# The second gate's modulation, computed in 64 small pieces on VectorE: each piece tied to its chunk's last low part, with four buffers and loads three chunks ahead

## The chip, the cores and the metric

The kernel runs on one core of one Trainium2 chip. The metric is the device time of one execution, in microseconds, so lower is better. The engines are called PE (TensorE's matrix products), PEld (its weight loads), DVE (VectorE), ACT (ScalarE), POOL (GpSimd) and SP (SyncE, which only issues transfers here). Each engine works through its own instructions in a fixed order.

## What is computed

One layer of a transformer-like block on x of shape 512 x 2048, with a feed-forward width of 5632, all in float32. The part that matters here is the modulation `mod`, a product of one vector with a 2048 x 12288 matrix that yields six vectors of 2048, and the end of the layer, where the sixth of them, gt2, multiplies the result of the feed-forward part.

```
c_act = jax.nn.silu(c)
...
mod = c_act @ w_ada[l] + b_ada[l]
sh1, sc1, gt1, sh2, sc2, gt2 = jnp.split(mod, 6, axis=-1)
h = modulate(rms_norm(x, g_mix[l]), sh1, sc1)
...                    # input projection, two head groups, output projection
x = x + gt1 * ...
h = modulate(rms_norm(x, g_ffn[l]), sh2, sc2)
...                    # up projection of width 2 x 5632, SiLU gate, down projection
x = x + gt2 * ...
```

## The kernel before, in words

The kernel goes through its stages one behind the other: the mixing part (until 742 us), two ordinary up units and 40 fast up units (742 to 1668 us), and the down projection (1668 to 2099 us). A product in float32 is made of three: every operand is split into a high part (made on ACT) and a low part (the rest, made on DVE), and PE computes high by high, high by low and low by high.

**Fast up units.** A unit uf{f}, f = 4 to 43, makes one 128-wide slice of the gate and of the up projection by a scheme of the Strassen kind with seven products where there would be eight. It consists of two chunks (c = 0, 1) with 84 matmuls each. `fast_chunk` prepares the weights of a chunk, uq{f}_{c}: SP loads them raw (L1037, `r`), ACT makes the high parts and DVE the low parts of four groups, named `a`, `c`, `s` and `t` in the order in which PE uses them (`ah`/`al` and so on; L229 and L230 in `wsplit`, L1043 and L1044 for `c`), and DVE makes the sums between them (L1046, L1047, L1050). The last low part of a chunk is `tl`. High and low parts of the groups a, s and t have three buffers each, so the weights are made about a chunk ahead of PE. At the end of a unit ACT copies one product from PSUM (L1083, uw), DVE combines the seven (L1084 to L1088), ACT applies SiLU (L1089), DVE multiplies gate and up (L1090, ug), and `keep_act` makes the combinations that the down projection needs (L961 to L964) and SP writes them to DRAM as td (L965 to L969). POOL meanwhile adds weight blocks of the down projection in DRAM (L977).

**The pieces of gt2.** The sixth modulation vector is spread over the fast up units from unit 12 on, one piece per chunk, 64 pieces in all (`gt2_piece`, called behind a chunk's matmuls are written). A piece is a load of 256 KB of the matrix (L173, on ACT's queue, so that it stands in line with ACT's high parts) and one operation on DVE that multiplies it by the vector c and adds up along each row (L182). The tiles have two buffers, and the load of piece n + 2 is written behind the operation of piece n. Behind the last piece, four small sums on DVE (L188, L190) put the four quarters together with the bias into `mod`. At the start of the down projection, `gt2_spread` turns the vector round: SP scatters it to DRAM as gt2d (L1152, 8 KB in elements of 4 bytes), and four broadcast loads bring it back as gt2b (L1156), which is first used near the end.

**Down projection.** Each chunk of a phase loads a block of weights (L1100, `dq…r`) and activations from td (L1115, `dq…tl`); ACT makes the high part of the activations (L1116, `th`) and of the weights (L229, `w0h`, `w1h`), and DVE the low parts (L1117, L230) and a sum of two weight blocks (L1122). In the first phase products 4 and 5 alternate, so two chunks share every name, such as dq_0tl: the first is product 4's and the second product 5's. PE's groups are called dn4, dn5 and so on.

**What sets the order.** A scheduler orders each engine's instructions by priority and dependencies. `tc.high_priority(offset=AHEAD)` raises the priority of what is written in it; weights of chunks ahead are written in it. `tc.issue_after(i)` makes an instruction stand behind instruction i. `tail_hi` and `tail_lo` are lists of ACT's high parts and DVE's low parts, to which `wsplit` appends; `tail_lo[-1]` is the last low part written so far, which at a piece is its chunk's `tl`.

Of the kernel before, what the change touches and what calls it, by code (L numbers as in the profile page):

```python
# [8 lines left out]
F32 = mybir.dt.float32  # L9
F32R = mybir.dt.float32r  # L10
AF = mybir.ActivationFunctionType
ALU = mybir.AluOpType
AX = mybir.AxisListType

P = 128
D = 2048
S = 512
KT = D // P
# [18 lines left out]
AHEAD = 2000  # L37
# [27 lines left out]
def block_kernel(ctx, tc, xT, crow, adaT, vecs, bfr, w1, wyr, wqkv0, wqkv, wgate, wout, wup0, wups, wdn, outT):  # L65
    nc = tc.nc
    PSUM = bass.MemoryType.PSUM
    cp = ctx.enter_context(tc.tile_pool(name="cp", bufs=1))
# [13 lines left out]
    def page(name, tag, shape=None):  # L82
        return pgp.tile(shape or [P, S], F32, tag=tag, name=name, bufs=TAGS[tag])
# [13 lines left out]
    c_b = cp.tile([P, D], F32, name="c_b")  # L97
# [69 lines left out]
    gt2_acc = cp.tile([P, 4, KT], F32, name="gt2_acc")  # L167
    gt2_src = {}

    def gt2_load(n):  # L170
        t = cp.tile([P, S], F32, name=f"gt2_{n}", tag="ssq", bufs=2)
        with tc.issue_after(tail_hi[-1]):
            nc.scalar.dma_start(out=t, in_=adaT[GT2 * KT + n // 4, :, (n % 4) * S:(n % 4 + 1) * S])  # L173
        gt2_src[n] = t

    def gt2_piece(n):
        if n == 0:
            gt2_load(0)
            gt2_load(1)
        t = gt2_src.pop(n)  # L180
        r = n % 4
        nc.vector.scalar_tensor_tensor(out=t, in0=t, scalar=1.0, in1=c_b[:, r * S:(r + 1) * S], op0=ALU.mult, op1=ALU.mult,  # L182
                                       accum_out=gt2_acc[:, r, n // 4:n // 4 + 1])
        if n < 4 * KT - 2:
            gt2_load(n + 2)
        if n == 4 * KT - 1:
            m = mods[GT2]
            nc.vector.tensor_add(m, gt2_acc[:, 0, :], vec[:, V_BADA + GT2 * KT:V_BADA + (GT2 + 1) * KT])  # L188
            for r in range(1, 4):
                nc.vector.tensor_add(m, m, gt2_acc[:, r, :])  # L190
# [7 lines left out]
    tail_lo, tail_hi = [], []  # L198
# [167 lines left out]
    for kt in range(KT):  # L366
# [3 lines left out]
        else:  # L370
# [3 lines left out]
                                       in1=bg[:, kt:kt + 1], op0=ALU.add, op1=ALU.add)  # L374
# [19 lines left out]
    for f in (4, 5, 6, 7, 0, 1, 2, 3):  # L394
        t = page(f"xr{f}", "c")
# [35 lines left out]
    for f in range(4):  # L431
        t = page(f"yr{f}", "c")
# [437 lines left out]
    for g in range(4):  # L870
# [12 lines left out]
        for f in range(4):  # L883
            kt = g * 4 + f
            t = page(f"x1_{kt}", "c")
# [173 lines left out]
    for f in range(2 * STD, FT):  # L1059
        ps = [bank(f + 1, b, f"uf{f}p{b}") for b in range(4)]  # L1060
        m = {p: ps[b][:, h * HS:(h + 1) * HS] for p, (b, h) in where.items()}
        for c in range(2):
            for p, hi, lo in fast_chunk(f, c):
                for k in range(4):
                    th, tl = T[p][c * 4 + k]
                    ks = slice(k * P, (k + 1) * P)
                    for n, (w, x) in enumerate(((hi, th), (hi, tl), (lo, th))):
                        first, last = c + k + n == 0, c == 1 and k == 3 and n == 2
                        nc.tensor.matmul(m[p], lhsT=R(w[:, ks]), rhs=R(x), start=first and p in opens, stop=last,  # L1069
                                         skip_group_check=True)  # L1070
            if f == 2 * STD and c == 0:
                up_last()
            n = 2 * (f - 2 * STD) + c
            if 0 <= n - GT2_AT < 4 * KT:
                gt2_piece(n - GT2_AT)
            if 0 <= n - SUMS_AT < 6 * NQ and (n - SUMS_AT) % 6 < 4:
                sums24((n - SUMS_AT) // 6, (n - SUMS_AT) % 6)
# [28 lines left out]
    def dn_chunk(ph, q, hold=False):  # L1106
        prods = PHASES[ph]
        out = {p: [] for p, _, _ in prods}
        with tc.high_priority(offset=AHEAD):
            raws, ts = [], []  # L1110
            for n, (p, blk, ix) in enumerate(prods):
                nm = f"dq{p}_{q}"
                raws.append(dn_load("raw2" if n or (len(prods) == 1 and q % 2) else "raw", blk, q, nm + "r"))
                tl, th = page(nm + "tl", "h"), page(nm + "th", "h")
                nc.sync.dma_start(out=tl, in_=td[ph][q][:, ix])  # L1115
                nc.scalar.activation(R(th), tl, AF.Copy)  # L1116
                nc.vector.tensor_sub(R(tl), tl, th)  # L1117
                ts.append((th, tl))
            for n, (p, blk, ix) in enumerate(prods):
                nm, raw = f"dq{p}_{q}", raws[n]  # L1120
                if n and blk >= 0:
                    nc.vector.tensor_add(raw, raw, raws[0])  # L1122
                for k in range(2):
                    if hold and n == 0:
                        w = []
                        for i in range(2):
                            src = raw[:, (2 * k + i) * S:(2 * k + i + 1) * S]
                            hi, lo = page(f"{nm}h{k}{i}", "h"), page(f"{nm}l{k}{i}", "h")
                            nc.scalar.activation(R(hi), src, AF.Copy)
                            nc.vector.tensor_sub(R(lo), src, hi)  # L1130
                            w.append((hi, lo))
                    else:
                        hi, lo = wsplit(raw[:, k * 1024:(k + 1) * 1024], 1024, f"{nm}w{k}")
                        w = [(hi[:, i * S:(i + 1) * S], lo[:, i * S:(i + 1) * S]) for i in range(2)]
                    ks = slice(k * HS, (k + 1) * HS)
                    out[p].append((w, ts[n][0][:, ks], ts[n][1][:, ks]))
        return out
# [45 lines left out]
    for ph, prods in enumerate(PHASES):  # L1183
# [4 lines left out]
        for q in range(NQ):  # L1188
            hold = ph == 3 and q >= NQ - 2
            out = dn_chunk(ph, q, hold)  # L1190
# [101 lines left out]
```

## Time and profile before

| | us |
|---|---|
| median of 3 runs | 2101.8 (2100.73 to 2103.46) |
| profiled execution | 2100.19 |
| its span, first to last instruction | 2098.5 |
| PE busy in the span | 2047.3 (98%) |
| DVE busy | 1709.0 (81%) |
| ACT busy | 939.6 (45%) |
| the 64 pieces on DVE (L182), busy | 43.9 |
| from the first unit with pieces (uf12) to the last (uf43) | 1004.77 to 1643.66 |

Times inside the profile count from the start of its span. A group's row reads: line, engine, operation, output <- input, shape, count, then busy us and mean ns of one, then idle time of the engine just ahead of these and what ended it. A row of the chain of waits reads: start, length, what. A row of the waits reads: who waited <- for whom: us in all, times, longest.

### The profile page before, as it was taken

Reading aid. Unit: us, or ns where it says so; the run is one execution under the profiler, and the core shown is the slowest. Engines: PE = TensorE matmul, PEld = TensorE weight load, DVE = VectorE, ACT = ScalarE, POOL = GpSimd, SP = SyncE. Lnnn points to the kernel's source line nnn. Section 1 sums busy time; section 2 is a strip of 40 time slices with the busy share of each in tenths; the row PEclk is TensorE's granted clock in tenths of the full one; section 3 lists DMA queues with packets and bytes.
Section 4 is the critical chain, followed back from the end, with each engine's and each line's share of the span. In section 5 each row is a group of like instructions: output and inputs, shape, how many; then the busy total and the mean of one; then the engine's idle time right before and its main releaser. Section 6 shows DMA issues by size and latency. Waiting matters only on the chain.

```text
span 2098.5 us, 32298 instructions
## 1 busy us (share of the span) xinstructions
PE 2047.3 (98%) x12529; PEld 1856.8 (88%) x12529; DVE 1709.0 (81%) x2547; ACT 939.6 (45%) x1331; POOL 92.6 (4%) x111
## 2 busy tenths in 40 slices
PE   8999999999999999999999999999999999999999
PEld 6889898888788887999999999999999888888877
DVE  8999768987776569988798897889898877777785
ACT  4433447765433355444343333343343445545443
POOL 0000000000100000000000000000000000000000
PEclk9999999999999999999999999999999999999999
DMA  9989766667667532448878788987878587677884
GB/s 339 354 290 317 247 204 209 232 212 255 229 229 265 201 131 78 141 134 221 243 226 236 233 233 222 251 245 220 246 230 228 164 280 249 233 244 249 275 303 151
DMA packets 174044, 485.21 MB, mean 231 GB/s; under 512 B 20385, under 2 KB 45377, under 8 KB 169794
## 3 DMA queue, kind: packets, MB, share of 16 engines
q1 hardware_dynamic: 154530, 429.66, 60.6%
q0 software_dynamic: 10144, 36.70, 9.4%
q10 hardware_dynamic: 9216, 16.78, 2.4%
q8 instruction: 98, 1.61, 0.3%
q14 instruction: 56, 0.46, 0.1%
HBM read 447.40 MB, written 93.35 MB: 258 GB/s over the span
## 4 chain that ended last, share of the span: by engine, by line
PE 73%; DVE 13%; DMA 9%; issue 2%; ACT 2%; POOL 1%; SPq 0%; ACTq 0%; DVEq 0%
PE w1p L234 4%; DMA gt<-in_adaT 3%; PE dn6p L234 3%; PE dn7p L234 3%; PE dn1p L234 3%; PE yr1p L234 2%; PE up0p L234 2%; PE wo2p L234 2%; PE wo1p L234 2%; PE wo3p L234 2%; PE dn3p L234 2%; PE dn5p L234 2%; PE wo0p L234 2%; PE dn2p L234 2%; PE yr0p L234 2%
## 5 line engine op out<-in xcount | busy, mean ns | idle before, releaser
L229 ACT ACTIVATE uq_0sh<-uq_0r 128x1024 fp32r<-128x1024 f32 x40 | 42.4, 1060 | 221.6 <-DVE uq_0r L1047 221.6
L154 DVE SCALAR_TENSOR_TENSOR ada<-ada,c_b 128x1024 f32<-128x1024 f32 x96 | 115.9, 1219 | 26.3 <-DMA ada<-in_adaT 26.1
L182 DVE SCALAR_TENSOR_TENSOR gt<-gt,c_b 128x512 f32<-128x512 f32 x64 | 43.9, 685 | 61.3 <-DMA gt<-in_adaT 61.3
L229 ACT ACTIVATE uq_1sh<-uq_1r 128x1024 fp32r<-128x1024 f32 x40 | 42.5, 1062 | 106.4 <-DVE uq_1r L1047 95.5
L977 POOL DMA_DIRECT2D s2d<-in_wdn x44 | 36.4, 827 | 692.0 <-DMA s2d<-in_wdn 674.7
L230 DVE TENSOR_TENSOR uq_0sl<-uq_0r,uq_0sh 128x1024 fp32r<-128x1024 f32 x40 | 49.0, 1225 | 17.3 <-ACT uq_0sh L229 15.9
L229 ACT ACTIVATE uq_0ah<-uq_0r 128x1024 fp32r<-128x1024 f32 x40 | 42.2, 1056 | 34.4 <-PE uf8p L1069 1.8
L230 DVE TENSOR_TENSOR uq_0al<-uq_0r,uq_0ah 128x1024 fp32r<-128x1024 f32 x40 | 48.8, 1220 | 7.5 <-ACT uq_0ah L229 7.3
L230 DVE TENSOR_TENSOR uq_0tl<-uq_0r,uq_0th 128x1024 fp32r<-128x1024 f32 x40 | 48.8, 1219 | 7.6 <-ACT uq_0th L229 7.6
L1089 ACT ACTIVATE ug<-ug 128x512 f32<-128x512 f32 x40 | 25.3, 632 | 62.8 <-DVE ug L1086 62.8
L234 PE MATMUL w1p<-hph,w1h 128*128 128x512 f32 x128 | 46.9, 395 | 5.9 <-ACT hph L378 5.9
L229 ACT ACTIVATE uq_1ah<-uq_1r 128x1024 fp32r<-128x1024 f32 x40 | 42.2, 1055 | 20.1 <-issue 15.5
L230 DVE TENSOR_TENSOR uq_1tl<-uq_1r,uq_1th 128x1024 fp32r<-128x1024 f32 x40 | 48.8, 1219 | 2.5 <-ACT uq_1th L229 2.5
L234 PE MATMUL w1p<-hpl,w1h 128*128 128x512 f32 x128 | 50.6, 395 | 0.0
L234 PE MATMUL w1p<-hph,w1l 128*128 128x512 f32 x128 | 50.3, 393 | 0.0
L230 DVE TENSOR_TENSOR uq_1sl<-uq_1r,uq_1sh 128x1024 fp32r<-128x1024 f32 x40 | 48.8, 1220 | 0.0
L1046 DVE TENSOR_TENSOR uq_0r<-uq_0r 128x1024 f32<-128x1024 f32 x40 | 48.7, 1217 | 0.0
L230 DVE TENSOR_TENSOR uq_1al<-uq_1r,uq_1ah 128x1024 fp32r<-128x1024 f32 x40 | 48.6, 1214 | 0.0
L1046 DVE TENSOR_TENSOR uq_1r<-uq_1r 128x1024 f32<-128x1024 f32 x40 | 48.5, 1213 | 0.0
L229 ACT ACTIVATE uq_0th<-uq_0r 128x1024 fp32r<-128x1024 f32 x40 | 41.9, 1048 | 12.9 <-DVE uq_0r L1050 3.0
L229 ACT ACTIVATE uq_1th<-uq_1r 128x1024 fp32r<-128x1024 f32 x40 | 42.0, 1051 | 9.7 <-PE uf10p L1069 1.0
L164 DVE SCALAR_TENSOR_TENSOR ada<-ada,c_b 128x1024 f32<-128x1024 f32 x32 | 38.9, 1216 | 2.0 <-DMA ada<-in_adaT 2.0
(12770 smaller groups left out, 8149.7 us busy)
## 6 DMA issues: line engine op xcount, KB each, us to landing
ada<-in_adaT SPq DMA_DIRECT2D x128, 512.0 KB, 5.0
uq_1r<-in_wups SPq DMA_DIRECT2D x80, 512.0 KB, 8.3
uq_0r<-in_wups SPq DMA_DIRECT2D x80, 512.0 KB, 4.9
s2d<-in_wdn POOLq DMA_DIRECT2D x44, 512.0 KB, 9.4
adf<-in_adaT SPq DMA_DIRECT2D x32, 512.0 KB, 5.9
gt<-in_adaT ACTq DMA_DIRECT2D x64, 256.0 KB, 4.6
s2d<-in_wdn SPq DMA_DIRECT2D x22, 512.0 KB, 8.4
s4d<-in_wdn SPq DMA_DIRECT2D x22, 512.0 KB, 8.5
```

The costliest lines, as they stand in the source:

```text
L154: nc.vector.scalar_tensor_tensor(out=t, in0=t, scalar=1.0, in1=cs, op0=ALU.mult, op1=ALU.mult, accum_out=ac)
L164: nc.vector.scalar_tensor_tensor(out=t, in0=t, scalar=1.0, in1=c_b[:, cs], op0=ALU.mult, op1=ALU.mult, accum_out=ada_acc[j][:, hf, i:i + 1])
L182: nc.vector.scalar_tensor_tensor(out=t, in0=t, scalar=1.0, in1=c_b[:, r * S:(r + 1) * S], op0=ALU.mult, op1=ALU.mult, accum_out=gt2_acc[:, ...
L229: tail_hi.append(nc.scalar.activation(R(hi[:, :n]), raw_ap, AF.Copy).ins)
L230: tail_lo.append(nc.vector.tensor_sub(R(lo[:, :n]), raw_ap, hi[:, :n]).ins)
L234: nc.tensor.matmul(ps, lhsT=R(l), rhs=R(r), start=start, stop=stop)
L977: nc.gpsimd.dma_start(out=out[:, cs], in_=src[:, cs], accum_op=ALU.add)
L1046: nc.vector.tensor_add(blocks[:, 0:3:2], blocks[:, 0:2], blocks[:, 2:3].broadcast_to([P, 2, 512]))
L1089: nc.scalar.activation(g, g, AF.Silu)
```

## The change

The tiles of the pieces take two tags by turns, with two buffers each, so there are four. Three loads are issued at the first piece, and the load of piece n + 3 is written ahead of the operation of piece n. The operation itself is written with high priority and is tied to stand behind the last low part that was written. Nothing else is edited.

```
     def gt2_load(n):
-        t = cp.tile([P, S], F32, name=f"gt2_{n}", tag="ssq", bufs=2)
+        t = cp.tile([P, S], F32, name=f"gt2_{n}", tag=("ssq", "rstd_b")[n % 2], bufs=2)
...
     def gt2_piece(n):
-        if n == 0:
-            gt2_load(0)
-            gt2_load(1)
+        for k in range(3 if n == 0 else 0):
+            gt2_load(k)
+        if n < 4 * KT - 3:
+            gt2_load(n + 3)
         t = gt2_src.pop(n)
         r = n % 4
-        nc.vector.scalar_tensor_tensor(out=t, in0=t, scalar=1.0, in1=c_b[:, r * S:(r + 1) * S], op0=ALU.mult, op1=ALU.mult,
-                                       accum_out=gt2_acc[:, r, n // 4:n // 4 + 1])
-        if n < 4 * KT - 2:
-            gt2_load(n + 2)
+        with tc.issue_after(tail_lo[-1]), tc.high_priority(offset=AHEAD):
+            nc.vector.scalar_tensor_tensor(out=t, in0=t, scalar=1.0, in1=c_b[:, r * S:(r + 1) * S], op0=ALU.mult,
+                                           op1=ALU.mult, accum_out=gt2_acc[:, r, n // 4:n // 4 + 1])
```

How this moves instructions is shown at two places. The first is DVE's order around the end of unit 15 (uq15_1 is its second chunk; sl and tl are the last two low parts of a chunk, al the first). Before:

```order
L230 TENSOR_TENSOR uq15_1sl_10350<-uq15_1r_10336,uq15_1sh_10349 128x1024
L182 SCALAR_TENSOR_TENSOR gt2_8_10332,gt2_acc_128<-gt2_8_10332,c_b_81 128x512
L230 TENSOR_TENSOR uq15_1tl_10355<-uq15_1r_10336,uq15_1th_10354 128x1024
L182 SCALAR_TENSOR_TENSOR gt2_9_10443,gt2_acc_128<-gt2_9_10443,c_b_81 128x512
L230 TENSOR_TENSOR uq16_0al_10478<-uq16_0r_10474,uq16_0ah_10477 128x1024
```

And now:

```order
L230 TENSOR_TENSOR uq15_1sl_10352<-uq15_1r_10338,uq15_1sh_10351 128x1024
L1090 TENSOR_TENSOR ug14_10211<-ug14_10211,uu14_10212 128x512
L230 TENSOR_TENSOR uq15_1tl_10357<-uq15_1r_10338,uq15_1th_10356 128x1024
L184 SCALAR_TENSOR_TENSOR gt2_7_10093,gt2_acc_128<-gt2_7_10093,c_b_81 128x512
L230 TENSOR_TENSOR uq16_0al_10480<-uq16_0r_10476,uq16_0ah_10479 128x1024
```

Two pieces stood around the second chunk's last low part; now one stands behind it, and the other (gt2_8) behind the next chunk's, so at this place the pieces are two numbers behind. The loads on ACT's queue stand a row or two earlier than before.

The second place is SP's order at the change from the up units to the down projection (gt2d is the scatter of the modulation vector; td_10 are the writes of the last units' activations). Before:

```order
L969 DMA td_10_6749<-tw_16773 128x256
L1152 DMA gt2d<-mod_127 128x16x1
L1115 DMA dq_0tl<-td_0_6717 128x512
L1100 DMA dq_1r<-in_wdn 128x1024 x2
L1115 DMA dq_0tl<-td_0_6717 128x512
L1115 DMA dq_1tl<-td_1_6718 128x512
L966 DMA td_10_6738<-ug_17009 128x256
L1100 DMA dq_1r<-in_wdn 128x1024 x2
L1115 DMA dq_1tl<-td_1_6718 128x512
L1115 DMA dq_2tl<-td_2_6719 128x512
```

And now:

```order
L1115 DMA dq_0tl<-td_0_6717 128x512
L1100 DMA dq_1r<-in_wdn 128x1024 x2
L1115 DMA dq_0tl<-td_0_6717 128x512
L1115 DMA dq_1tl<-td_1_6718 128x512 x2
L1100 DMA dq_1r<-in_wdn 128x1024 x2
L1115 DMA dq_2tl<-td_2_6719 128x512
L966 DMA td_10_6738<-ug_17009 128x256
L1152 DMA gt2d<-mod_127 128x16x1
L1115 DMA dq_2tl<-td_2_6719 128x512
L1115 DMA dq_3tl<-td_3_6720 128x512
```

The scatter moved from ahead of the first activation load to a place behind five activation loads and two pairs of weight loads, right ahead of product 5's dq_2tl. On DVE the last piece and the last of its sums moved too: the piece stood ahead of unit 43's first low part and the last sum shortly behind that; both stand behind its last low part now.

## The prediction

> **What bounds the kernel now.** I read the page's totals first, then busy time by stretch, the chain of waits, the waits of PE and DVE, and last the timelines around the two places that looked odd.
>
> ```profile
> span 2098.5 us, 32298 instructions
> ...
> PE 2047.3 (98%) x12529; PEld 1856.8 (88%) x12529; DVE 1709.0 (81%) x2547; ACT 939.6 (45%) x1331; POOL 92.6 (4%) x111
> ...
> L182 DVE SCALAR_TENSOR_TENSOR gt<-gt,c_b 128x512 f32<-128x512 f32 x64 | 43.9, 685 | 61.3 <-DMA gt<-in_adaT 61.3
> ```
>
> PE is busy 98% of the span, so only idle PE time or slow PE time can be won. The last row is what the change touches: 64 pieces on DVE, 0.685 us each, with 61.3 us of DVE idle in front of them, all of it waiting for their loads. DVE is not the bound over the whole span, so the question is how much of the 61.3 reaches PE. The next view gives busy time by stretch (start:end and length; PE, PEld, DVE, ACT, POOL; granted clock, DMA share, GB/s): the pieces run in the first stretch, the second runs from the last fast up unit to the end of the down stage's first phase.
>
> ```profile
> 1004.77:1643.66 638.89, 630.31 (x5211) 627.26 (x5210) 557.27 (x815) 251.68 (x310) 49.20 (x60) 1.00 0.83 234
> 1643.66:1790.31 146.65, 142.66 (x698) 120.36 (x697) 113.41 (x110) 71.70 (x88) 0.00 (x0) 0.99 0.72 236
> 1295.00:1300.00 5.00, 4.69 (x27) 4.69 (x28) 4.45 (x6) 2.16 (x3) 0.00 (x0) 0.66 0.23 59
> 1300.00:1305.00 5.00, 5.00 (x44) 5.00 (x43) 4.93 (x8) 2.22 (x4) 0.00 (x0) 1.00 0.59 182
> ```
>
> The chain of waits (start, length, what) tells how long an undisturbed unit is, and where the chain leaves PE:
>
> ```profile
> 984.62 20.16 PE uf11p L1069 x168
> ...
> 1018.74 10.82 DMA gt<-in_adaT
> ...
> 1087.74 20.16 PE uf16p L1069 x168
> ...
> 1284.60 8.80 DMA gt<-in_adaT
> 1295.31 21.62 PE uf26p L1069 x166
> ...
> 1643.66 2.79 PE uf43p L1069 x24
> 1646.45 9.88 DMA dq_0tl<-td
> ...
> 1790.31 5.44 PE dn1p L234 x24
> ```
>
> A fast up unit without a wait takes 20.16 us. Units 12 to 42 are 31 units, 31 x 20.16 = 624.96 us, and the stretch took 638.89: **13.9 us too long**. Of that, 638.89 - 630.31 = 8.6 us is PE idle, and 5.3 us is PE busy but slow, as in 1295 to 1300 where the clock was 0.66. Who made PE wait there (us in all, times, longest), and what DVE waited for:
>
> ```profile
> PE uf26p L1069 <- DVE uq_0al L230: 2.3, 1, 2.3
> PE uf43p L1069 <- ACT uq_1sh L229: 1.5, 1, 1.5
> PE uf20p L1069 <- DVE uq_0al L230: 1.4, 1, 1.4
> PE uf14p L1069 <- DVE uq_0al L230: 1.1, 1, 1.1
> PE uf43p L1069 <- DVE uq_1sl L230: 0.8, 1, 0.8
> ```
> ```profile
> DVE gt L182 <- DMA gt<-in_adaT: 61.3, 20, 5.5
> ```
> ```profile
> 1293.42 0.69 DVE L182 SCALAR_TENSOR_TENSOR gt<-gt,c_b 128x512 f32<-128x512 f32 x1 [5.47 <-DMA gt<-in_adaT]
> ```
>
> The low part uq_0al that PE misses is the instruction right behind such a piece. The load was issued at 1284.60, and DVE reached the piece at 1293.42 - 5.47 = 1287.95: a lead of 3.3 us for a load that took 8.8. So 20 late loads stop DVE, and where DVE's lead over PE is used up PE stops too, and is slow for some us after. The units just ahead of the pieces, such as uf11, show no excess, so I put all 13.9 us down to these loads.
>
> **The change, part by part.**
>
> *Loads three ahead, four buffers.* The number of loads and their bytes stay; they stay on ACT's queue, a row or two earlier there. By the order, the load now stands about two and a half chunks ahead of its piece: 2.5 x 10.08 (half of 20.16) = 25 us. The longest wait for one in the chain was 10.82 us, from its issue at 1018.74. A load of piece n+3 needs the buffer of piece n-1, which by then is over a chunk old, so ACT's queue, with the weights' high parts in it, gets no wait. The 20 waits of DVE should go. Value: the whole 13.9 us. The bounds: 8.6 if only PE's idle time went and matmuls stayed slow, 13.9 if all goes. I take 13.9, since the clock row shows full speed again 5 us after the wait, so the slowness belongs to it.
>
> *The piece behind the chunk's last low part.* Both pieces of a unit stood around the second chunk's last low part; now each stands behind its own chunk's. The instruction count is the same: 64 x 0.685 us. What matters is whether it stands ahead of something that PE needs soon. An undisturbed unit:
>
> ```profile
> 1098.33 1.23 DVE L230 TENSOR_TENSOR uq_1sl<-uq_1r,uq_1sh 128x1024 fp32r<-128x1024 f32 x1
> ...
> 1100.68 1.22 DVE L230 TENSOR_TENSOR uq_1tl<-uq_1r,uq_1th 128x1024 fp32r<-128x1024 f32 x1
> ```
> ```profile
> 1102.22 0.28 PE L1069 MATMUL uf16p<-td4h,uq_1sl 128*128 128x256 f32 x1
> ...
> 1105.10 0.28 PE L1069 MATMUL uf16p<-te4h,uq_1tl 128*128 128x256 f32 x1
> ```
>
> uq_1sl was ready at 1099.56 and needed at 1102.22 (2.7 us to spare); uq_1tl at 1101.90 and 1105.10 (3.2 us). The new order puts one piece, the first chunk's, ahead of uq_1sl, at most +0.685 us, and leaves uq_1tl with one piece ahead of it as before (the other one); both fit. DVE is 557.27 / 638.89 = 87% busy with unchanged work, so it keeps up. Cost: 0. The cover is those 2.7 us; if it were gone, each chunk would pay up to 0.685.
>
> *What follows the last piece.* Four small sums into the modulation, then SP scatters it to DRAM (L1152) and reads it back, broadcast. The last piece stands a unit later in DVE's order (behind unit 43's last low part, where it stood ahead of unit 43's first), so the scatter moves on SP too: from ahead of the down stage's first activation load to behind seven of its loads (five of activations, two of weight blocks). Before, the scatter did this:
>
> ```profile
> 1641.67 0.37 SPq L1152 DMA_DIRECT2D gt2d<-mod  x1
> 1646.45 0.32 SPq L1115 DMA_DIRECT2D dq_0tl<-td  x1
> ```
> ```profile
> DMA packets 2742, 1.17 MB, mean 234 GB/s; under 512 B 2074, under 2 KB 2586, under 8 KB 2742
> ```
> ```profile
> 1644.00:1646.00 2.00, 2.00 (x19) 2.00 (x18) 2.00 (x2) 0.08 (x1) 0.00 (x0) 1.00 0.56 1
> 1646.00:1648.00 2.00, 2.00 (x19) 2.00 (x18) 1.90 (x4) 0.91 (x1) 0.00 (x0) 1.00 0.01 0
> ...
> 1652.00:1654.00 2.00, 2.00 (x19) 2.00 (x18) 0.12 (x1) 0.00 (x0) 0.00 (x0) 1.00 0.51 44
> 1654.00:1656.00 2.00, 2.00 (x19) 2.00 (x19) 0.00 (x0) 0.00 (x0) 0.00 (x0) 1.00 1.02 202
> ```
> ```profile
> 1657.08 0.69 DVE L1117 TENSOR_TENSOR dq_0tl<-dq_0tl,dq_0th 128x512 fp32r<-128x512 f32 x1 [4.96 <-ACT dq_0th L1116]
> ```
>
> The packet row is of 1640 to 1645: 2074 packets under 512 B, of which 16 x 128 = 2048 are the scatter's elements. From 1644 to about 1653, some 8 us, hardly a byte moves, and dq_0tl, issued 4.8 us behind the scatter, lands at 1646.45 + 9.88 = 1656.33, 14.7 us after the scatter. ACT and DVE stand behind it in their order (4.96 us), and PE waits twice in uf43 (1.5 + 0.8):
>
> ```profile
> 1662.00:1664.00 2.00, 2.00 (x12) 2.00 (x11) 2.00 (x3) 0.48 (x1) 0.00 (x0) 0.54 0.41 125
> ```
> ```profile
> 1667.78 0.63 PE L234 MATMUL dn4p<-dq_0w0h,dq_0th 128*128 128x512 f32 x2
> ...
> 1674.95 0.47 PE L234 MATMUL dn5p<-dq_0w0h,dq_0th 128*128 128x512 f32 x1 [1.18 <-DVE ug L1086]
> ```
>
> The first down matmul starts 1667.78 - 1643.66 = 24.12 us after unit 43, 3.96 above 20.16: 2.3 us of waits and 1.66 of slow clock (0.54). With the scatter gone from there, 3.96 us are saved. What is late next is the load behind the scatter's new place. DVE's rows up to the last sum, without the 4.96 us wait, end near 1662 on the old clock; the scatter goes out then. Product 5's dq_2tl is right behind it: it lands between 1674 (when the old gap began to fill, 12 us) and 1676.7 (14.7 us); I take 1675.5. On ACT the high part of the second half of dn5's first chunk (dq_0w1h) stands behind that load's own high part in the new order; the two cost
>
> ```profile
> 1670.15 0.62 ACT L1116 ACTIVATE dq_2th<-dq_2tl 128x512 fp32r<-128x512 f32 x1
> 1670.72 1.06 ACT L229 ACTIVATE dq_0w1h<-dq_0r 128x1024 fp32r<-128x1024 f32 x1
> ```
>
> so 0.62 + 1.06 us later, 1677.2, PE can go on. It gets there earlier: dn5 at 1674.95 - 4.0 = 1670.9, its second half (half of 5.44) at 1673.6. A stall of 3.6, with 1.66 of slow clock as in uf43: 5.3. Net of the transition: +5.3 - 4.0 = **+1.3 us**. Bounds: -4.0 if the scatter hurts nobody there, +5.3 if a second wait like uf43's (3.96) follows in the next chunk.
>
> By the Trainium skill's page DMA: Bandwidth & Descriptors, section Bandwidth, a packet has a floor of about 10.5 ns; 2,048 of them on 16 engines would be an estimate of 1.3 us, and by it the transition would be -4.0. The trace speaks against it, with 8 us without data.
>
> *Sum.* Against the profiled execution (span 2098.5, with what lies around it 2100.19): 2100.19 - 13.9 + 1.3 = 2087.6. The runs' median, 2101.8, is 1.6 above that execution, so I forecast 2101.8 - 13.9 + 1.3 = **2089.2 us**.
>
> **The rivals.**
>
> *The scatter is hidden in its new place.* For it: SP now loads ahead, seven loads are through, and PE has dn4's chunk to work on. Against it: dq_2th and dq_0w1h stand in ACT's fixed order. 2101.8 - 13.9 - 4.0 = 2083.9.
>
> *Loads stay late in part.* For it: DMA share is 0.83 in that stretch, with a load of 10.8 us; bursts could be longer where a POOL accumulation runs. Half of the 13.9 stays: 2101.8 - 7.0 + 1.3 = 2096.1.
>
> *The change doesn't do what it says.* The load is tied to the place in ACT's order; were the DVE piece to move ahead with it, the lead would stay at 3 us and PE's waits with it: 2101.8 + 0 to 1.3. Against it: the order shows the lead.
>
> *Slower: the piece on the weights' path.* If DVE had no lead left behind the last low part, each of 64 pieces would be paid by PE: 64 x 0.685 = 43.8, less 13.9, less 4.0: 2127.7. It decides once the 2.7 us to spare are used up; in the undisturbed unit they are not.
>
> A rule on the clock bears on the price of a wait: the Trainium skill, TensorE: Matmul & The Clock Gate, Part 1, has PE fall to half rate after an idle window of about 3.4 us. Here the wait of 2.3 us in uf26 already shows 0.66, and the two in uf43, 2.3 together, 0.54, so this trace goes below that rule; by it the short stalls would cost their length only, and the new one 3.6.
>
> **How the numbers follow.** The forecast 0.58; scatter hidden 0.21; half the waits 0.08; no effect 0.08; slower 0.05. The forecast's own range is 2086 to 2094, the transition's bounds less what is unlikely. The range goes down to the hidden scatter (2083) and up to the half (2096), and leaves out no effect and slower. A time counts as changed from 0.2%, or 4.2 us, about what a measurement of this kernel can tell: faster 0.58 + 0.21 + 0.08 = 0.87, same 0.08, slower 0.05.
>
> **What would show it.** Right: no DVE idle ahead of the pieces, units 12 to 42 at 625 us, uf43 at 20.2, a PE wait in dn5's first chunk, behind dq_0w1h. Wrong: waits of PE for low parts in the up stage, DVE idle at the pieces, or more than 22 x 5.44 + 7 us in the down stage's first phase.

## The result, and the profile after

| | before, us | changed, us |
|---|---|---|
| median of the runs (6 each) | 2101.27 (2096.96 to 2103.46) | 2086.04 (2082.36 to 2090.33) |
| ratio | | 0.9931 (95%: 0.9914 to 0.9947) |
| span of the profiled execution | 2098.5 | 2084.2 |

The change makes the kernel 0.7% faster, 11 to 18 us by the interval. The forecast was 2089.2, within 2083 to 2096. The table by stretch shows a gain and, against it, a loss (first the stretch of units 12 to 42, then unit 43 to the end of the first down phase; start:end and length, then PE, PEld, DVE, ACT, POOL, granted clock, DMA share, GB/s):

```profile
1001.89:1626.85 624.96, 624.96 (x5211) 624.96 (x5210) 558.21 (x808) 264.42 (x310) 49.21 (x60) 1.00 0.84 239
1626.85:1776.90 150.05, 143.21 (x698) 119.92 (x697) 114.28 (x118) 71.77 (x89) 0.00 (x0) 0.98 0.72 232
```

The first took 638.89 us and takes 624.96, which is 31 x 20.16: PE is never idle in it. The second took 146.65 and takes 150.05. So -13.93 and +3.40. The waits of PE, which before were a list of missed low parts, have none left in the up units with pieces, and a new one at the head (the view from 840 us on):

```profile
PE dn5p L234 <- ACT dq_0w1h L229: 5.0, 1, 5.0
PE dn2p L234 <- DVE dq_5w1l L230: 1.2, 1, 1.2
PE dn4p L234 <- DVE dq_0w1l L230: 0.6, 1, 0.6
PE dn5p L234 <- DVE dq_2w0l L230: 0.6, 1, 0.6
PE dn5p L234 <- DVE ug L1086: 0.6, 1, 0.6
```

The row of the pieces among the costliest groups has the same busy time as before, and no idle time ahead of it (it was 61.3):

```profile
L184 DVE SCALAR_TENSOR_TENSOR gt<-gt,c_b 128x512 f32<-128x512 f32 x64 | 43.8, 684 | 0.0
```

The chain of waits runs through unit 43 undisturbed and leaves PE right behind it, for the load behind the scatter. SP's timeline has the two issues, ACT's and PE's what waited:

```profile
1626.85 20.13 PE uf43p L1069 x168
1646.99 13.34 DMA dq_2tl<-td
```
```profile
1646.52 0.38 SPq L1152 DMA_DIRECT2D gt2d<-mod  x1
1646.99 2.40 SPq L1115 DMA_DIRECT2D dq_2tl<-td  x1
```
```profile
1660.35 0.63 ACT L1116 ACTIVATE dq_2th<-dq_2tl 128x512 fp32r<-128x512 f32 x1 [10.28 <-DMA dq_2tl<-td]
1660.89 1.04 ACT L229 ACTIVATE dq_0w1h<-dq_0r 128x1024 fp32r<-128x1024 f32 x1
```
```profile
1661.98 1.22 PE L234 MATMUL dn5p<-dq_0w1h,dq_0th 128*128 128x512 f32 x2 [5.02 <-ACT dq_0w1h L229]
```

The scatter goes out at 1646.52 and the load behind it lands at 1646.99 + 13.34 = 1660.33; ACT stands 10.28 us at that load's high part, with the weights' high part that PE needs next behind it, and PE stands 5.02 us. The clock falls with it, to half at 1659, 2.0 us after PE stopped:

```profile
1656.00:1658.00 2.00, 0.96 (x5) 0.45 (x3) 0.00 (x0) 0.00 (x0) 0.00 (x0) 1.00 0.77 24
1658.00:1660.00 2.00, 0.00 (x0) 0.00 (x0) 0.00 (x0) 0.00 (x0) 0.00 (x0) 0.75 0.70 183
1660.00:1662.00 2.00, 0.02 (x1) 0.02 (x1) 0.04 (x1) 1.65 (x3) 0.00 (x0) 0.50 1.04 400
```
```profile
1658.50:1659.00 0.50, 0.00 (x0) 0.00 (x0) 0.00 (x0) 0.00 (x0) 0.00 (x0) 0.99 0.78 143
1659.00:1659.50 0.50, 0.00 (x0) 0.00 (x0) 0.00 (x0) 0.00 (x0) 0.00 (x0) 0.50 0.70 225
```

The two stretches give -10.5 us; the spans differ by 14.3. The other 3.8 lie outside them: 2.9 ahead of unit 12, where the change edits nothing, and 0.9 behind the first down phase. Unit 12 starts anywhere between 1001.7 and 1010.0 us in the profiles shown here and below, so the 2.9 are within the scatter of single executions; that the change has no part in the 0.9 is not shown.

### The profile page after: what moved, and what is told of

Its sections match the earlier page's. It is cut to its first block, busy times and chain, and to the rows that moved or that the text cites. A ratio compares the mean times of both kernels' runs of the same rounds, so it can differ in the third digit from the quotient of the medians.

```text
span 2084.2 us, 32340 instructions
## 1 busy us (share of the span) xinstructions
PE 2041.7 (98%) x12529; PEld 1854.4 (89%) x12529; DVE 1710.0 (82%) x2547; ACT 951.2 (46%) x1331; POOL 91.7 (4%) x111
## 4 chain that ended last, share of the span: by engine, by line
PE 84%; DVE 8%; DMA 4%; issue 1%; ACT 1%; POOL 1%; SPq 0%; DVEq 0%; ACTq 0%
PE w1p L234 4%; PE dn6p L234 3%; PE dn7p L234 3%; PE dn1p L234 3%; PE dn5p L234 2%; PE dn3p L234 2%; PE dn2p L234 2%; PE yr1p L234 2%; PE up0p L234 2%; PE wo2p L234 2%; PE wo3p L234 2%; PE wo1p L234 2%; PE dn4p L234 2%; PE yr0p L234 2%; PE wo0p L234 2%; PE h3p L234 2%
```

## The experiments

All stage times are from one profile per kernel, counted from the first matmul of unit 12, of unit 43, of dn4 and of dn1 (before, by this count, unit 43 to dn4 took 24.28; by the chain's rows 24.12). A ratio is to the kernel before on the same chip.

| kernel | units 12 to 42 | unit 43 to dn4 | unit 43 to dn1 | ratio |
|---|---|---|---|---|
| before | 638.89 | 24.28 | 146.65 | 1 |
| changed | 624.96 | 20.16 | 150.05 | 0.9931 (0.9914 to 0.9947) |
| e1, piece tied alone | 624.96 | 20.16 | 150.49 | 0.9935 (0.9915 to 0.9955) |
| e2, buffers and loads alone | 636.91 | 25.09 | 149.63 | 1.0012 (0.9993 to 1.003) |
| e3, pieces from chunk 12 | 624.96 | 20.16 | 142.83 | 0.9895 (0.9857 to 0.9932) |
| e4, scatter in rows | 624.96 | 20.16 | 141.92 | |
| e5, pieces from chunk 14 | 624.96 | 29.75 | 151.03 | |
| e6, scatter on ACT's queue | 624.96 | 20.16 | 148.79 | |
| e7, tied, one load ahead | 624.96 | 20.16 | 151.52 | |
| e8, two operations per piece | 624.96 | 20.15 | 152.15 | |
| e9, changed again | 624.96 | 20.16 | 152.50 | 0.9927 (0.9914 to 0.9941) |
| e10, as e3, again | 624.96 | 20.15 | 143.54 | 0.9895 (0.9883 to 0.9908) |
| e11, before, from chunk 14 | 641.44 | 21.14 | 144.47 | |

**Which part of the change brings the gain.** e1 keeps two buffers and the load two ahead, and ties the operation, with its high priority:

```
     (kernel before)
-        nc.vector.scalar_tensor_tensor(out=t, in0=t, ...
+        with tc.issue_after(tail_lo[-1]), tc.high_priority(offset=AHEAD):
+            nc.vector.scalar_tensor_tensor(out=t, in0=t, ...
```

> The kernel before with one part of the change: the piece is tied behind its chunk's last low part with high priority; two buffers and the load of piece n + 2 written behind piece n, as before. In the order the load then stands 1.67 chunks (16.8 us) ahead of its piece, against 0 to 0.67 before and 3.0 with the whole change. Theory A (what counts is the distance that tying the piece gives; a load needs at most about 10.5 us): DVE idles ahead of pieces under 3 us in all, units 12 to 42 take 625 to 626 us, the whole time is within 2 us of the changed kernel's, about 2086. Theory B (the four buffers and the third load ahead carry the gain): units 12 to 42 stay at 634 us or more, the time above 2095.

e2 is the other half:

```
     (changed kernel)
-        with tc.issue_after(tail_lo[-1]), tc.high_priority(offset=AHEAD):
-            nc.vector.scalar_tensor_tensor(out=t, in0=t, ...
+        nc.vector.scalar_tensor_tensor(out=t, in0=t, ...
```

> The changed kernel with the piece not tied and without priority: four buffers and loads three pieces ahead alone. In the order the pieces move forward with the loads, to one or two numbers earlier than their chunk, and the distance from load to piece is 0 to 0.67 chunk, as before. Theory A: DVE still idles about 60 us ahead of pieces, units 12 to 42 take 634 to 642 us, no gain there; the scatter is issued early, ahead of dq_0tl as before, or a little earlier. Theory B: units 12 to 42 at 625 to 628 us.

The stretch of units 12 to 42 in e1, and in e2 (the same view), and what DVE waits for in e2:

```profile
1005.10:1630.06 624.96, 624.96 (x5211) 624.96 (x5209) 558.70 (x809) 264.40 (x310) 49.20 (x60) 1.00 0.84 239
```
```profile
1004.68:1641.59 636.91, 629.22 (x5211) 625.89 (x5209) 558.19 (x817) 251.59 (x310) 49.20 (x60) 1.00 0.84 235
```
```profile
DVE gt L183 <- DMA gt<-in_adaT: 57.7, 20, 5.2
```

Theory A, in both. Tying the operation (tie and priority together; they were not tried apart) brings the whole 13.9 us; four buffers with loads three ahead, alone, leave DVE waiting 57.7 us in 20 waits, as before, and their ratio is 1.0012. A third load ahead doesn't help by itself because the order of DVE isn't tied to it: with more buffers the pieces, which nothing holds, stand one or two numbers earlier in DVE's order, and the distance from load to piece stays at 0 to 0.67 chunk. In time, DVE reaches the 20 pieces that wait 3.1 to 7.4 us after their load's issue in e2, and 3.3 to 6.4 us after it in the kernel before.

e7 asks how little distance will do, with the piece tied and a single load ahead:

```
     (e1's kernel)
         if n == 0:
             gt2_load(0)
-            gt2_load(1)
...
-        if n < 4 * KT - 2:
-            gt2_load(n + 2)
+        if n < 4 * KT - 1:
+            gt2_load(n + 1)
```

> As the run with the piece tied alone, two buffers, but with one load ahead instead of two. In the order the load then stands one chunk (10.1 us) ahead of its piece, about the longest landing seen (10.5 us; median 5.9). Theory A (the distance from load to piece against the time of a load decides): DVE waits for a few loads, under 10 us in all, each by under 2 us, and PE, which has 2.7 us to spare, loses under 1 us: units 12 to 42 at 625 to 626 us. Theory B (a depth of three or four buffers is needed): 630 us or more.

```profile
1009.96:1634.92 624.96, 624.96 (x5211) 624.96 (x5209) 558.22 (x809) 264.41 (x310) 49.21 (x60) 1.00 0.85 239
```

```profile
DMA to landing us min/median/max: 2.5/5.7/9.1
```

The view of DVE's waits has no row for a piece's load, so one chunk of distance in the order is enough; even the waits that were expected did not come. In time that distance is more than the 10.1 us of a chunk: in this trace the median piece starts 12.3 us after its load's issue, and the longest landing is 9.1 us (the row above, of the pieces' loads). The depth of the change, four buffers and three chunks, is more than was needed.

**Whether the pieces cost anything where they stand.** e8 adds a second operation behind each piece:

```
     (changed kernel, behind the operation of the piece)
+        with tc.issue_after(tail_lo[-1]), tc.high_priority(offset=AHEAD):
+            nc.vector.scalar_tensor_tensor(out=t, in0=c_b[...], scalar=1.0, in1=c_b[...], ...,
+                                           accum_out=gt2_x[:, n % 4:n % 4 + 1])
```

> The changed kernel with a second operation of the same size on DVE behind each piece, whose result is not used: it doubles the DVE work of the pieces, 64 x 0.684 = 44 us more, and takes no load. Theory A (a piece behind the last low part is hidden in DVE's slack, 2.7 us per half unit; DVE goes from 89% to 96%): units 12 to 42 at 625 to 628 us. Rival D (the piece stands on the weights' path): every added operation is paid, 625 + 44 = 669 us, or at least 640. The scatter goes out later in this kernel, so the stretch behind unit 43 isn't compared.

```profile
1007.80:1632.76 624.96, 624.96 (x5211) 624.96 (x5210) 587.00 (x930) 260.82 (x310) 49.21 (x60) 1.00 0.85 239
```

```profile
L188 DVE SCALAR_TENSOR_TENSOR gt<-c_b 128x512 f32<-128x512 f32 x62 | 42.3, 683 | 0.0
```

The 62 added operations that fall in the stretch take 0.683 us each, 42.3 us in all (the second row). DVE's busy time there counts records that overlap only once and rises by 28.8 us, to 94%. PE loses nothing. The pieces are hidden, with room to spare.

**What the scatter costs.** e3 moves the pieces four chunks forward, and the scatter with them:

```
-    GT2_AT, SUMS_AT = 16, 14
+    GT2_AT, SUMS_AT = 12, 14
```

> The changed kernel with the first piece four chunks earlier (chunk 12 in place of 16), so that the last piece and the scatter stand about 40 us ahead of the change to the down projection, among loads with some 25 us to spare. Theory A (the scatter costs only through what stands right behind it): no wait of PE in dn5's first chunk, the stretch from unit 43 to the end of the first down phase falls from 150.05 to 142 to 144 us, the time to about 2079. Rival C (the stall in dn5's first chunk is of the stage's own, for instance a page or a write of td that comes late): the stretch stays at 148 us or more.

e4 leaves the scatter where the change put it, but lays its 8 KB down row by row; what comes back as gt2 is then in another order, so the turning of the vector is left out:

```
-        nc.sync.dma_start(out=gd.rearrange("k p -> p k"), in_=mods[GT2])
+        nc.sync.dma_start(out=gd.rearrange("k p -> (k p)").rearrange("(p k) -> p k", k=KT), in_=mods[GT2])
```

> The changed kernel with the scatter in the same place and with the same 8 KB, written row by row (128 runs of 64 bytes in place of 2048 of 4 bytes), which leaves out turning the vector round. Theory A (the 2048 elements hold the transfers up for some 8 us or more): the load behind it lands within about 6 us of its issue, not 13.3, no 5 us wait in dn5's first chunk, the stretch from unit 43 to the end of the first down phase at 142 to 145 us. Rival C: 148 us or more.

The stretch from unit 43 on in e3 and in e4, and e4's issues on SP with the use of the load on ACT:

```profile
1632.63:1775.46 142.83, 140.71 (x699) 119.06 (x697) 113.17 (x111) 72.24 (x89) 0.00 (x0) 1.00 0.73 244
```
```profile
1626.99:1768.91 141.92, 140.68 (x698) 119.07 (x697) 114.62 (x118) 72.38 (x89) 0.00 (x0) 1.00 0.72 245
```
```profile
1645.40 0.32 SPq L1152 DMA_DIRECT2D gt2d<-mod  x1
1645.81 0.38 SPq L1115 DMA_DIRECT2D dq_2tl<-td  x1
```
```profile
1651.05 0.64 ACT L1116 ACTIVATE dq_2th<-dq_2tl 128x512 fp32r<-128x512 f32 x1 [2.11 <-DMA dq_2tl<-td]
```

How long the scatter itself takes is in the rows of the DMA issues (KB, then us from issue to landing), in the changed kernel and in e4:

```profile
gt2d<-mod SPq DMA_DIRECT2D x1, 8.0 KB, 11.7
```
```profile
gt2d<-mod SPq DMA_DIRECT2D x1, 8.0 KB, 2.3
```

Theory A in both: 150.05 becomes 142.83 with the scatter early, and 141.92 with the same bytes in rows at the same place; the load behind it is used 5.2 us after its issue there, not 13.3. It is the 2048 elements of four bytes that cost, 7 to 8 us of PE's time here. Two details of e3's expectation were missed: a wait of 1.5 us stays in dn5's first chunk, for an operation of the up stage on DVE (ug), and the time was 2082.4 and not 2079. Also, the first piece of e3 waits 5.6 us for its load, which costs PE 1.3 us in unit 10, ahead of the stretches compared here.

e5 and e11 move the scatter in the other kernels' places, by `GT2_AT = 14` in the changed kernel and in the kernel before:

> The changed kernel with the first piece two chunks earlier (chunk 14). In SP's order the scatter then stands right ahead of the first dq_0tl again, where it stood in the kernel before; all else is as in the changed kernel. Theory A (the scatter delays by some 14 us whatever stands right behind it on SP): the 5.0 us wait in dn5's first chunk goes, and waits of 1.5 to 3 us in unit 43 come back, with the first down matmul 23 to 25 us after unit 43's start (20.1 in the changed kernel); stretch from unit 43 to the end of the first down phase 145 to 148 us. Rival C (unit 43's waits of before came from late pieces, not from the scatter): first down matmul 20.1 to 20.5 us after unit 43's start.

> The kernel before with the pieces two chunks earlier and nothing else, so that the scatter stands among the last weight loads of the up units and not right ahead of dq_0tl. Theory A (the scatter alone held up unit 43): the first down matmul 20.2 us after unit 43's start in place of 24.1, the stretch from unit 43 to the end of the first down phase 142 to 144 us in place of 146.65, while units 12 to 42 keep about 14 us of waits, less about 1 for the two chunks that move ahead of the stretch. Rival C: the first down matmul stays at 24 us.

e5's rows on SP and PE's waits:

```profile
1634.31 0.38 SPq L1152 DMA_DIRECT2D gt2d<-mod  x1
1634.78 1.19 SPq L1115 DMA_DIRECT2D dq_0tl<-td  x1
```
```profile
PE uf43p L1069 <- ACT uq_1sh L229: 6.2, 1, 6.2
PE dn5p L234 <- DVE ug L1086: 1.2, 1, 1.2
PE uf43p L1069 <- DVE uq_1sl L230: 0.5, 1, 0.5
```

In e5 the stall leaves dn5 and comes back in unit 43, at the very instructions that waited in the kernel before. Its size was missed: 29.75 us to the first down matmul, not 23 to 25, and 151.03 for the stretch, not 145 to 148. The scatter goes out 3.0 us after the first matmul of unit 43 here (1634.31 against 1631.26), and in the kernel before 1.8 us ahead of it, so about the same delay reaches farther (dq_0tl is used 14.5 us after the scatter's issue here, and landed 14.7 us after it before). In e11 unit 43 is nearly free (21.14; 20.2 was expected), the stretch falls to 144.47, and the waits of the up units stay (641.44, 16.5 us too long where 13 were expected). The 3.96 us that the prediction put down to the scatter were its doing but for about 1 us.

e6 asks what is held up, SP's queue or the transfers as a whole:

```
-        nc.sync.dma_start(out=gd.rearrange("k p -> p k"), in_=mods[GT2])
+        nc.scalar.dma_start(out=gd.rearrange("k p -> p k"), in_=mods[GT2])
```

> The changed kernel with the scatter issued on ACT's queue in place of SP's, between two high parts of about the same time. Theory A1 (what is held up is SP's own queue, in whose order the 2048 elements stand): the load of product 5's dq_2tl lands within 7 us of its issue and PE waits under 2 us in dn5's first chunk; stretch from unit 43 to the end of the first down phase 142 to 146 us. Theory A2 (the transfer engines are held up, whichever queue it comes from): dq_2tl takes 12 us or more and the stretch is 148 to 152 us.

ACT's timeline around the scatter, SP's, the windows behind it, and PE's longest wait in the stretch:

```profile
1648.26 0.42 ACTq L1152 DMA_DIRECT2D gt2d<-mod  x1
1648.78 1.06 ACT L229 ACTIVATE dq_0w1h<-dq_0r 128x1024 fp32r<-128x1024 f32 x1 [3.67 <-DVE mod L190]
...
1652.69 0.63 ACT L1116 ACTIVATE dq_2th<-dq_2tl 128x512 fp32r<-128x512 f32 x1 [0.75 <-DMA dq_2tl<-td]
...
1659.23 0.63 ACT L1116 ACTIVATE dq_3th<-dq_3tl 128x512 fp32r<-128x512 f32 x1 [4.96 <-DMA dq_3tl<-td]
```
```profile
1647.78 0.38 SPq L1115 DMA_DIRECT2D dq_2tl<-td  x1
1648.26 0.45 SPq L1115 DMA_DIRECT2D dq_3tl<-td  x1
```
```profile
1652.00:1654.00 2.00, 2.00 (x10) 1.66 (x9) 2.00 (x3) 1.31 (x2) 0.00 (x0) 1.00 1.01 11
1654.00:1656.00 2.00, 2.00 (x10) 1.41 (x8) 2.00 (x5) 0.27 (x1) 0.00 (x0) 1.00 0.29 8
1656.00:1658.00 2.00, 2.00 (x9) 1.66 (x10) 1.59 (x3) 0.00 (x0) 0.00 (x0) 1.00 0.71 55
```
```profile
PE dn4p L234 <- ACT dq_1w1h L229: 2.3, 1, 2.3
```

Neither expectation holds as written. Product 5's dq_2tl lands in time, but only because SP, with no scatter of its own to wait for, issues it at 1647.78, half a microsecond ahead of the scatter. The load that SP issues with the scatter, dq_3tl at 1648.26, is used 11 us later, and 8 to 55 GB/s move from 1652 to 1658. PE's wait moves a chunk on, to the weights' high part behind dq_3tl's (2.3 us). So a queue of its own does not let SP's loads through, which speaks for A2; the stretch, 148.79, is 1.3 us better than the changed kernel's, perhaps by the load that got ahead, though the changed kernel's own two profiles differ by 2.5 (150.05 and e9's 152.50). Where in the transfer engines the hold-up lies was not tried.

**A version that beats both.** e9 and e10 time the changed kernel and e3 side by side:

> The changed kernel itself, timed beside the next one on one chip. Ratio to the kernel before 0.991 to 0.995; stages as in its profile: units 12 to 42 at 624.96 us, from unit 43 to the end of the first down phase 150 us.

> The changed kernel with the pieces four chunks earlier, once more, for its distance to the changed kernel on the same chip. Theory A: the 7.2 us that its profile showed in the stretch from unit 43 to the end of the first down phase (142.8 against 150.0), so a ratio to the kernel before that is 0.003 to 0.004 below that of the changed kernel. If the earlier scatter takes as much elsewhere, the two ratios agree within 0.001.

Medians 2088.77 and 2081.21 us against 2104.08 of the kernel before on that chip, ratios 0.9927 (0.9914 to 0.9941) and 0.9895 (0.9883 to 0.9908). The intervals don't touch. The medians differ by 7.6 us, and the profiles by 9.0 us in the stretch from unit 43 on (152.50 and 143.54), so the early scatter takes back little elsewhere. e9's 152.50, where 150 was expected, shows how far this stretch varies from one execution of the changed kernel to another: its wait for dq_0w1h was 5.3 us, and two shorter ones in the first chunks 1.3 us each, where they were 0.6 and less.

## Why the prediction was right, point by point

- *The loads, -13.9 us.* Right in size: 638.89 to 624.96. Right that the distance from load to piece is what counts, but the gain was put down to the wrong half of the change: the prediction names loads three ahead and four buffers as what brings the distance, and gives the place of the piece no gain. e1 and e2 show that the tie brings it alone, and e7 that one chunk of it is enough. The number came out all the same because both halves were in the change. The prediction's own rival, a piece that moves ahead with its load, is what e2 shows without the tie. By the trace the loads lead by 32 us (median), not 25, which changes nothing.
- *The piece behind the last low part, 0.* Right: 624.96 with the pieces, and still 624.96 with a second operation of 0.683 us behind each (e8). The rival of pieces on the weights' path is out.
- *Unit 43 freed, -4.0.* Right: 20.16 in place of 24.28, which is -4.1; e11 puts all but about 1 us of it down to the scatter.
- *The stall in dn5's first chunk, +5.3.* The right place (dq_0w1h behind product 5's dq_2th) and the right cause, but too small: the time from dn4's start to the end of the phase rose from 146.65 - 24.28 = 122.37 to 150.05 - 20.16 = 129.89, by 7.5 us. Counted from unit 43's start, PE reached the place at 30.1 (forecast 29.9), and the load landed at 33.5 (31.8 by the forecast's 1675.5). Most of that is the scatter's issue, at 19.7 in place of 18.3: ahead of the last sum DVE waited 1.49 us for ACT's high part of another activation load (the row below, of DVE's timeline), which the forecast had not counted. The flight was 13.8 us, where 13.5 was taken between 12 and 14.7. So the wait was 5.0 and not 3.6, and slow matmuls and small waits behind it took 2.5 and not 1.7.

```profile
1640.47 0.69 DVE L1117 TENSOR_TENSOR dq_0tl<-dq_0tl,dq_0th 128x512 fp32r<-128x512 f32 x1 [1.49 <-ACT dq_0th L1116]
```

- *The transition in sum, +1.3.* Mis-sized: +3.40 in this profile, within the stated bounds of -4.0 and +5.3, and 152.50 - 146.65 = +5.9 in e9's, a little outside them. One of the prediction's signs of being wrong came true: more than 22 x 5.44 + 7 = 126.7 us in the first down phase, where 129.89 were measured. The sign was drawn too tight, since the forecast's own stall on top of the phase before gives 122.4 + 5.3 = 127.7, but it points at the right term, the transition, which cost more than was allowed for.
- *The sum.* -10.5 by the two stretches, where -12.6 was forecast; the medians differ by 15.2 us (15.3 with e9). Of the 4.7 us between, 3.8 lie outside the two stretches, and the profiled run before is 1.1 us faster than its median, the changed one 0.1. Whether the change has a part in them is open: the stretch of units 12 to 42 varies with unlucky loads in kernels that keep the waits (636.91 to 641.44), and the changed kernel's doesn't. With the transition's measured +3.4 the prediction's sum would have been 2101.8 - 13.9 + 3.4 = 2091.3, so its 2089.2 came nearer to 2086.04 than its terms deserve.
- *The rival that the scatter is hidden* is out: 13.8 us to the next landing here, 14.7 before. Had it been hidden, the stretch from unit 43 on would have been e3's or e4's, 142.8 or 141.9. By the Trainium skill's page DMA: Bandwidth & Descriptors, section Bandwidth, the estimate for the store was 1.3 us; the page gives its figure for loads issued from GpSimd, and the division by 16 engines is the prediction's own. The trace doesn't agree: the store lands 11.7 us after its issue.
- *The clock.* In the 5.0 us wait here the clock is at half from 1659.0 on, 2.0 us after PE stopped at 1656.96. In uf26 before, PE stopped at 1292.96, and the row below has the clock fall inside its half microsecond, some 2.2 us later. By the Trainium skill, TensorE: Matmul & The Clock Gate, Part 1, the clock falls after an idle window of about 3.4 us. Neither wait agrees with it: in both the clock fell sooner. So the prediction was right to price a short stall above its length.

```profile
1295.00:1295.50 0.50, 0.19 (x1) 0.19 (x2) 0.50 (x2) 0.00 (x0) 0.00 (x0) 0.71 0.96 213
```

## What to carry to other kernels

In this kernel, loading further ahead helped only with the operation that uses the load held back: ask how far apart issue and use stand in the two engines' orders, not how many buffers there are. When idle time goes, follow what was queued behind it: a later last piece moved a small store onto the path, and the start of the pieces, one number, was worth another 7 us. A store like this one, in single elements, should be issued where the loads behind it have some 19 us to spare, by the latest load that is reported below.

## What the hardware showed that was not expected

An 8 KB store in 2048 elements of 4 bytes lands 11.5 to 12.8 us after its issue in the profiles that give it (changed, e1, e5 to e9), and the same bytes in 128 runs of 64 bytes in 2.3 us (e4). Loads behind it come late. One issued right behind it is used 13.8 to 14.5 us after the store's issue (changed, e1, e5, e7, e9), and one issued with it on another queue after 11 us (e6). Loads that are issued later are still held up: those issued 4.8, 7.5 and 8.1 us behind the store came 14.7 (before), 17.6 (e6) and 18.3 us (e2) after the store's issue. The rows of e2:

```profile
1638.02 0.58 SPq L1151 DMA_DIRECT2D gt2d<-mod  x1
```
```profile
1646.11 10.24 DMA dq_0tl<-td
```

The same 8 KB in rows delays nothing that shows: 5.2 us from the next load's issue to its use.
